# Norms, value projections and a modulation group around the layer boundary of a two-layer diffusion mixer

## The chip, the cores and the metric

The kernel runs on one core of a Trainium2 chip. The metric is the device time of one execution in microseconds (us), taken as the median over runs. Engines by their short names: PE is TensorE's matmul, PEld its weight load, DVE is VectorE, ACT is ScalarE, POOL is GpSimd, SP is SyncE, which here only issues transfers (DMAs).

## The reference, cut to what matters

Two layers, 512 tokens of 1024 channels (four tiles of 128 tokens; tiles 0 and 1 are context, 2 and 3 latent). Each layer is a token mixer (latent attention beside a chunkwise mLSTM, then an output projection) and a mixture of experts (MoE), each with a residual and a norm behind it:

```python
for l in range(DEPTH):
    sh1, sc1, g1, sh2, sc2, g2 = split(silu(c) @ w_ada[l] + b_ada[l], 6)
    y = token_mixer(layer_norm(x) * (1 + sc1) + sh1, ...)
    x = layer_norm(ALPHA * x + g1 * y, ln1_g, ln1_b)
    y = hier_moe(layer_norm(x) * (1 + sc2) + sh2, ...)
    x = layer_norm(ALPHA * x + g2 * y, ln2_g, ln2_b)
```

So between layer 0's MoE and layer 1's mixer every tile is normalised twice: by the post-norm ln2, and by the norm without gains that opens the next mixer. In the mixer the normalised input h is multiplied by columns of w_in; among them are 256 columns called kr here (keys' rest, rotary part and gates), 512 of the mLSTM's values (mv), its keys and queries (mk, mq), and others (kd, qd, po, gates of the branches). The gates of the mLSTM need the kr columns of all tiles.

## The kernel before

All is f32; products with w_in are made of three matmuls on high and low parts (`mm3`), for which weights and activations are split: the high part by a Copy on ACT, the low part by a subtraction (`sub`, L157) that goes to POOL each third time and to DVE otherwise (`split_sb`, L162; `wsplit`, L452, for weights). One tile of tokens by 256 columns takes 24 matmuls (`tm`, L537); `cm` (L547) gives 128 columns by all tokens.

The program's planner orders the instructions of each engine at build time, by their place in the text and by when a simulated operand and buffer are there; only PE's order in the MoE loop is as written. Each engine and each DMA queue then works in order. Weights pass through the W slots: four of 1 MB in the pool `wp`, taken whole by `wm` (L207) or as two halves by `w` (L198); in the MoE `wm` goes round these four and seven more (W2, layer 0) of the MoE's own pool. Tiles with tag `u` (34 in layer 1) and `hT` belong to the mixer's pool, whose memory the MoE's pool used before; `st` (12) and `pm` (4) are there for the whole program.

The end of the MoE (`moe`, L1548 to L1575): ln2's gains are loaded into a `wm` slot; for each tile in turn the combine adds the last experts (L1466, L1469, with sums), the mean is formed (L1560), `stats` (L1475) squares on ACT (L1480, result into the MoE's tile xr) and makes the inverse root on DVE: `newton` (L143) guesses through integer bits and improves three times, seven operations behind one for the argument (L1481). Two passes over the tile apply it (L1562, L1569). For layer 0 the second norm's mean and `stats` follow, and L1574 leaves r and nb. Then ada(1,1) is run (L1577), a third of layer 1's modulation: `ada(l, g)` (L355) loads 16 pieces of w_ada (L377), makes 32 products on PE (L381; 64 rows of the trace), adds a bias (L387) and stores the rows (L392). `late` means whole W slots and an order of loads as written.

The start of layer 1's mixer (L484 to L514): the kr columns are loaded and split, ada(1,2) is begun, and for each tile ACT makes xn (L492), PE turns it (L495), scale and shift are put on (L508, L510), h is split (L511, L512), and one eighth of ada(1,2) is done. After this come kr's products for all tiles (L559), the gates' first part, mk and mq (L567), the values (`mv_cols`, L582) while the gates' second part runs, and then the mLSTM (`mlstm`, L848) in ten steps, into which `weave` puts the other columns (`fill`) and, in layer 0 only, ada(0,1) and ada(0,2) (`fill2`, L670).

Of the kernel before, what the change touches and what calls it, by code (L numbers as in the profile page):

```python
# [16 lines left out]
D = 1024  # L17
NCTX = 256
T = 512
NT = 4  # L20
# [63 lines left out]
class Kern:  # L84
# [77 lines left out]
    def split_sb(self, src, name="s", weights=False):  # L162

        n = 1
        for s in src.shape[1:]:
            n *= s
        pn = src.shape[0]
        hi, lo = self.pair(n, name, weights)

        def view(t):  # L170
            v = t[0:pn]
            if len(src.shape) == 3:
                v = v.rearrange("p (a b) -> p a b", a=src.shape[1])
            return v

        self.nc.scalar.activation(view(hi), src, AF.Copy)  # L176
        self.sub(view(lo), src, view(hi).bitcast(F32))
        return view(hi), view(lo)
# [134 lines left out]
    def setup(self):  # L313
# [25 lines left out]
        self.ada_d = [self.dp.tile([2, 6 * D], F32, name=f"ada{l}") for l in range(L)]  # L339
        self.zeros = self.cp.tile([128, 1], F32, name="zeros")  # L340
# [14 lines left out]
    def ada(self, l, g, late=False):  # L355

        nc, I = self.nc, self.I
        wv = I["w_ada"][l].rearrange("(p k) n -> k p n", k=8)
        ps = self.ps("d")

        def bias():
            bt = self.pm(name="bada") if late else (self.u(name="bada") if first else self.w("bada")[:, 0:512])
            for c in range(4):
                a = g * 2048 + c * 512
                nc.sync.dma_start(out=bt[32 * c:32 * c + 32], in_=I["b_ada"][l, a:a + 512].partition_broadcast(32))
            return bt

        first = l == 0 and g == 0
        bt = bias() if first else None
        for kb in range(8):  # L370
            if late:
                t = self.wm("wada")
                wt = self.halves2(t)
            else:
                wt = [self.w("wada") for c in range(2)]
            for c in range(2):
                d = nc.sync.dma_start(out=wt[c], in_=wv[kb][:, g * 2048 + c * 1024:g * 2048 + c * 1024 + 1024])  # L377
                if late:
                    self.tc.keep_in_program_order(d)
            for c in range(4):  # L380
                nc.tensor.matmul(ps[32 * c:32 * c + 32], lhsT=self.sT[:, kb],  # L381
                                 rhs=wt[c // 2][:, (c % 2) * 512:(c % 2) * 512 + 512],
                                 start=(kb == 0), stop=(kb == 7))
            if kb < 7:
                yield
        bt = bias() if bt is None else bt
        nc.vector.tensor_tensor(out=bt, in0=ps, in1=bt, op=OP.add)  # L387
        if g == 0:
            self.ada_cols(l, bt)
        for r in range(2):  # L390
            dst = self.ada_d[l][r:r + 1, g * 2048:g * 2048 + 2048].rearrange("o (c n) -> (o c) n", c=4)
            (nc.gpsimd if l else nc.sync).dma_start(out=dst, in_=bt[r:128:32])  # L392
        yield
# [58 lines left out]
    def wsplit(self, vs, cols=None):  # L452

        res = []
        for v in vs:
            if cols is not None:
                v = v[:, :, cols]
            nk, n = v.shape[1:]
            step = 512 // n
            for k in range(0, nk, step):  # L460
                m = min(step, nk - k)
                h, lo = self.split_sb(v[:, k:k + m], "ws", True)
                res += [(h[:, i], lo[:, i]) for i in range(m)]
        return res

    def mixer(self, l):
# [10 lines left out]
        hl = mp.tile([128, 8, 512], F32R, tag="hT", name="hTl", bufs=2)  # L477
        xT = {}
        if l == 0:
            ada0 = self.ada(0, 0)  # L480
            next(ada0)
        else:

            vkr = self.load_cols(win, 512, 160, (2208, 96))  # L484
            wkr = self.wsplit(vkr)
            ada0 = self.ada(1, 2)
        for t in range(NT):
            r, nb = self.nlx[t] if l else self.ln_scale(self.X[t])
            ts = slice(t * 128, t * 128 + 128)
            for g in range(2):  # L490
                xn = (self.u if l else self.st)(name="xn")
# [21 lines left out]
                next(ada0)  # L513
        run(ada0)  # L514
        if l == 0:
            tc.keep_in_program_order(nc.sync.dma_start(out=self.cst, in_=I["cst"][:, C_CAPF:]))
# [20 lines left out]
        def tm(v, toks, ws=None):  # L537

            ws = ws or self.wsplit(v)
            n = v[0].shape[2]  # L540
            for t in toks:
                p = self.ps("g")
                s = slice(t * 128, t * 128 + 128)
                self.mm3(p[:, 0:n], [(hh[:, k, s], hl[:, k, s], ws[k][0], ws[k][1]) for k in range(8)])
                yield t, p

# [9 lines left out]
        krg = self.sm([128, NT, 48], "krg", bufs=1)  # L556
        kd2 = [self.u(name="kd") for i in range(2)]
        kd = {t: kd2[t // 2][:, (t % 2) * 256:(t % 2) * 256 + 256] for t in range(NT)}
        for t, p in tm(vkr, range(NT), wkr):  # L559
            nc.scalar.activation(kd[t][:, 128:256], p[:, 0:128], AF.Copy)  # L560
            nc.vector.tensor_copy(krg[:, t], p[:, 128:176])
# [5 lines left out]
        for dst, c0, t0, n, sc in ((mk, 928, 0, T, 1.0), (mq, 672, q0, nq, 0.125)):  # L567
            v = self.load_cols(win, c0, 256)
            for b in range(2):
# [6 lines left out]
        V1 = [mp.tile([128, self.UW], F32, tag="u", name="v1", bufs=self.NU).rearrange("p (a b) -> p a b", a=NT)  # L576
              for h in range(4)]
        tpo = [self.u(name="tpo").rearrange("p (a b) -> p a b", a=4) for h in range(4)]
        for h in range(4):
            nc.gpsimd.memset(V1[h][:, :, 128:129], 1.0)  # L580

        def mv_cols():  # L582
            for c in range(2):
                v = self.load_cols(win, 1184 + c * 256, 256)
                for t, p in tm(v, range(NT)):
                    for i in range(2):
                        nc.scalar.activation(V1[2 * c + i][:, t, 0:128], p[:, i * 128:i * 128 + 128], AF.Copy)
                    yield
# [70 lines left out]
        for _ in range(4):  # L659
            next(fill)  # L660
# [9 lines left out]
        fill2 = self.chain(*[self.ada(0, g) for g in (1, 2)]) if l == 0 else iter(())  # L670
        mlstm = self.mlstm(l, QT, gates, mq, mk, V1, tpo, hmT)
        self.weave(mlstm, 10, [(fill, 32 if last else 34), (fill2, 16)])
# [611 lines left out]
    def moe(self, l):  # L1284
# [190 lines left out]
        def stats(X, nm, eps):  # L1475

            v, a, r = (self.ss_tile([128, 2], x) for x in "var")
            q, v, a, r = v[:, 1:2], v[:, 0:1], a[:, 0:1], r[:, 0:1]
            xi[0] += 1
            nc.scalar.activation(xrs[xi[0] % 3], X, AF.Square, bias=nm, accum_out=q)  # L1480
            nc.vector.tensor_scalar(v, q, 0.5 / D, 0.5 * eps, op0=OP.mult, op1=OP.add)  # L1481
            self.newton(r, v, a)
# [65 lines left out]
        ln2 = self.wm("ln2")  # L1548
# [4 lines left out]
        sums = {t: sm([128, 3], "sum", bufs=n) for t in QT}  # L1553
        comb = combine(done, sums)
        for t in QT:
# [4 lines left out]
            nc.vector.tensor_scalar(nm, sums[t][:, 0:1], sums[t][:, 1:2], -1.0 / D, op0=OP.add, op1=OP.mult)  # L1560
            r = stats(X, nm, EPS / ALPHA ** 2)
            nc.vector.scalar_tensor_tensor(X, X, nm, lg, op0=OP.add, op1=OP.mult)  # L1562
            if last:
# [4 lines left out]
                continue  # L1568
# [3 lines left out]
            nc.vector.tensor_scalar(nm, s2, -1.0 / D, None, op0=OP.mult)  # L1572
            r = stats(X, nm, EPS)
            nc.vector.tensor_tensor(out=nb, in0=nm, in1=r, op=OP.mult)  # L1574
            self.nlx[t] = (r, nb)  # L1575
        if not last:
# [19 lines left out]
```

## Time and profile before

| | |
|---|---|
| median of 3 runs | 1433.42 us (1429.83 to 1434.53) |
| the profiled execution | 1433.49 us, its span 1431.7 us |
| mean granted clock of TensorE | 0.947 |
| busy: PE, DVE, ACT, POOL | 1290.5, 798.3, 450.0, 379.9 us |
| moved by DMA | 339.66 MB, mean 237 GB/s |
| one w_ada piece, one wide w_in piece | 512 KB each |

The span is from the first to the last instruction; times in rows count from its start. Layer 0's mixer runs to some 530, its MoE to 826, layer 1's mixer to some 1150, its MoE to the end. In rows of windows the busy times come in the order PE, PEld, DVE, ACT, POOL; a clock of 1.00 is 2.4 GHz, 0.50 is 1.2 GHz. In timelines a row can stand for several equal instructions (x count), and brackets hold the idle time before it and what ended it. A matmul's length in the rows is modelled and overlaps the next one; distances between starts say more.

### The profile page before, as it was taken

The numbers are of one execution on the slowest core, as the hardware profiler recorded it, in microseconds if no ns is written. First come the engines' busy times: TensorE is split into PE (matmuls) and PEld (weight loads), VectorE is DVE, ScalarE is ACT, GpSimd is POOL, SyncE is SP. The second block draws the span as 40 slices with busy tenths as digits, with TensorE's granted clock in tenths as the row PEclk, the third lists the DMA queues.
The fourth block names the chain that finished last, engine by engine and source line by source line (L and its number), as shares of the span: only waits on it lengthen the run. The fifth ranks groups of instructions, "written<-read, shape, count | busy, mean of one in ns | idle before, by whom it ended". The sixth has DMA issues, their size and how long they took to land. (4 is left out here: it accounts for less than half of the span.)

```text
span 1431.7 us, 19677 instructions
## 1 busy us (share of the span) xinstructions
PE 1290.5 (90%) x6839; PEld 832.9 (58%) x6839; DVE 798.3 (56%) x2197; ACT 450.0 (31%) x998; POOL 379.9 (27%) x389
## 2 busy tenths in 40 slices
PE   5799999999999837899999969999999749999995
PEld 1688866776776633434454516998878634444442
DVE  2645777553236955555554486478775863343325
ACT  3434344343340102111121127356545212121121
POOL 1410114100342402444343312112524401232222
PEclk9999999999999958999999979999999959999998
DMA  9634454311257376979999968321444768999994
GB/s 327 205 96 148 140 200 126 99 44 60 89 176 269 131 289 228 404 278 409 408 407 409 404 211 281 96 79 40 152 143 133 232 252 329 408 408 407 407 408 156
DMA packets 146036, 339.66 MB, mean 237 GB/s; under 512 B 21552, under 2 KB 67792, under 8 KB 145920
## 3 DMA queue, kind: packets, MB, share of 16 engines
q1 hardware_dynamic: 137376, 322.87, 61.8%
q0 software_dynamic: 6096, 10.05, 2.0%
q10 hardware_dynamic: 2448, 5.31, 1.1%
q8 instruction: 59, 0.97, 0.3%
q14 instruction: 57, 0.47, 0.1%
HBM read 344.62 MB, written 4.29 MB: 244 GB/s over the span
## 5 line engine op out<-in xcount | busy, mean ns | idle before, releaser
L1426 PE MATMUL ps_g<-we,xs 128*64 128x512 f32 x992 | 240.1, 609 | 6.5 <-DMA we<-in_w_e_up 4.2
L160 POOL TENSOR_TENSOR wsl<-wc,wsh 128x512 fp32r<-128x512 f32 x55 | 73.9, 1346 | 326.9 <-ACT wsh L176 287.1
L1426 PEld LDWEIGHTS ps_g<-we,xs 128*64 128x64 f32 x992 | 75.3, 140 | 145.7 <-issue 139.0
L1472 POOL TENSOR_TENSOR X<-X,acc 128x512 f32<-128x512 f32 x96 | 125.1, 1326 | 110.2 <-DVE acc L1466 110.2
L160 DVE TENSOR_TENSOR wsl<-wc,wsh 128x512 fp32r<-128x512 f32 x107 | 86.8, 815 | 98.2 <-ACT wsh L176 78.2
L176 ACT ACTIVATE wsh<-wc 128x512 fp32r<-128x512 f32 x162 | 99.0, 628 | 120.3 <-PE ps_g L197 81.3
L1430 DVE SCALAR_TENSOR_TENSOR si<-si,ws,ps_g 128x256 f32<-128x256 f32 (+1 forms) x33 | 15.8, 480 | 205.6 <-ACT si L1429 205.6
L1449 PE MATMUL ps_a<-we,hidT 128*64 128x512 f32 x496 | 125.6, 595 | 3.2 <-DMA we<-in_w_e_down 3.1
L196 PE MATMUL ps_g<-wsh,hTh 128*128 128x256 f32 x400 | 115.2, 290 | 6.1 <-ACT hTh L533 3.1
L1382 POOL DMA_INDIRECT xr<-h2d,ti x33 | 34.8, 1055 | 312.2 <-PE ps_t L1394 203.6
L198 PE MATMUL ps_g<-wsh,hTl 128*128 128x256 f32 x400 | 113.3, 286 | 4.2 <-DVE hTl L160 4.1
L196 PE MATMUL ps_g<-hTh,wsh 128*128 128x512 f32 (+1 forms) x320 | 112.8, 352 | 1.9 <-ACT tg L627 1.9
L197 PE MATMUL ps_g<-wsl,hTh 128*128 128x256 f32 x400 | 113.7, 286 | 0.0
L197 PE MATMUL ps_g<-hTl,wsh 128*128 128x512 f32 (+1 forms) x320 | 111.1, 347 | 0.0
L198 PE MATMUL ps_g<-hTh,wsl 128*128 128x512 f32 (+1 forms) x320 | 110.4, 345 | 0.0
L381 PE MATMUL ps_d<-wada,sT 128*32 128x512 f32 x380 | 69.1, 641 | 30.4 <-DMA wada<-in_w_ada 15.4
L1466 DVE TENSOR_TENSOR acc<-ps_d,g 128x512 f32<-128x512 f32 x108 | 74.0, 689 | 38.1 <-PE ps_d L1464 24.3
L1429 ACT ACTIVATE si<-ps_g 128x256 f32<-128x256 f32 (+1 forms) x33 | 12.7, 384 | 241.5 <-PE ps_g L1426 186.4
L1463 PE MATMUL ps_d<-yh,pmr 128*128 128x512 f32 (+1 forms) x200 | 83.2, 417 | 1.2 <-DVE acc L1466 0.9
L196 PEld LDWEIGHTS ps_g<-wsh,hTh 128*128 128x128 f32 x400 | 76.6, 192 | 13.3 <-ACT hTh L533 3.4
L1449 PEld LDWEIGHTS ps_a<-we,hidT 128*64 128x64 f32 x496 | 38.4, 137 | 77.7 <-issue 61.0
L1464 PE MATMUL ps_d<-yl,pmr 128*128 128x512 f32 (+1 forms) x200 | 79.4, 398 | 0.9 <-DVE yl L190 0.9
(404 smaller groups left out, 2677.3 us busy)
## 6 DMA issues: line engine op xcount, KB each, us to landing
we<-in_w_e_gate SPq DMA_DIRECT2D x124, 512.0 KB, 10.2
we<-in_w_e_up SPq DMA_DIRECT2D x124, 512.0 KB, 10.5
we<-in_w_e_down SPq DMA_DIRECT2D x124, 512.0 KB, 10.2
wada<-in_w_ada SPq DMA_DIRECT2D x95, 512.0 KB, 6.5
wc<-in_w_in SPq DMA_DIRECT2D x63, 512.0 KB, 4.7
wc<-in_w_out SPq DMA_DIRECT2D x16, 512.0 KB, 5.7
wc<-in_w_bo_mla SPq DMA_DIRECT2D x8, 512.0 KB, 4.7
wc<-in_w_bo_mlstm SPq DMA_DIRECT2D x6, 512.0 KB, 3.5
```

The lines of the kernel that those rows point to most:

```text
L160: eng.tensor_tensor(out=out, in0=a, in1=b, op=OP.subtract)
L176: self.nc.scalar.activation(view(hi), src, AF.Copy)
L196: self.nc.tensor.matmul(out, lhsT=ah, rhs=bh, start=(i == 0), stop=False)
L197: self.nc.tensor.matmul(out, lhsT=ah, rhs=bl, start=False, stop=False)
L198: self.nc.tensor.matmul(out, lhsT=al, rhs=bh, start=False, stop=(i == n - 1))
L381: nc.tensor.matmul(ps[32 * c:32 * c + 32], lhsT=self.sT[:, kb], rhs=wt[c // 2][:, (c % 2) * 512:(c % 2) * 512 + 512], start=(kb == 0), sto ...
L1426: nc.tensor.matmul(p[64 * e:64 * e + 64], lhsT=xs[:, k, 64 * e:64 * e + 64], rhs=W[e, k], start=(k == 0), stop=(k == 7))
L1449: nc.tensor.matmul(p[64 * e:64 * e + 64], lhsT=hT_[:, c, 64 * e:64 * e + 64], rhs=W[e, c, h], start=(c == 0), stop=(c == 1))
L1463: nc.tensor.matmul(p, lhsT=lt, rhs=yh[h][0:m], start=(j == 0), stop=False)
L1464: nc.tensor.matmul(p, lhsT=lt, rhs=yl[h][0:m], start=False, stop=(j == len(parts) - 1))
L1466: nc.vector.tensor_tensor(out=a, in0=p, in1=g2[t // 2][h], op=OP.mult)
L1472: nc.gpsimd.tensor_tensor(out=X, in0=X, in1=a, op=OP.add)
```

## The change

- Roots: `stats` takes Sqrt on ACT, then a reciprocal and two DVE operations (one Newton step) in place of the guess and three steps. Its squares go to a bf16 tile of tag `st`.
- The norms become a generator for each tile (`norm`), in steps. In layer 0's MoE only the first steps are called; the others are called in the next mixer, between the starts of the tiles. For this ln2 lies in a W slot of `wp` and the sums in a lasting pool, and xn takes `st` tiles.
- In layer 1, kr's and the values' columns are loaded at the start, the values' sixteen split tiles lie in `u` with all low parts on POOL, and each tile's kr and value products follow its own start (`from_start`). `mv_cols` then does nothing in layer 1.
- ada(1,2) is taken from the start of the mixer and woven into the mLSTM as `fill2`, eight steps over ten. The bias loads of the late ada(1,1) are issued by POOL.

```diff
-    def split_sb(self, src, name="s", weights=False):
+    def split_sb(self, src, name="s", weights=False, pool=False):
...
-        self.sub(view(lo), src, view(hi).bitcast(F32))
+        if pool:
+            self.nc.gpsimd.tensor_tensor(out=view(lo), in0=src, in1=view(hi).bitcast(F32), op=OP.subtract)
+        else:
+            self.sub(view(lo), src, view(hi).bitcast(F32))
...
+        self.eps = {}
+        for e in (EPS, EPS / ALPHA ** 2):
+            self.eps[e] = self.cp.tile([128, 1], F32, name=f"eps{len(self.eps)}")
+            nc.gpsimd.memset(self.eps[e], e)
...
-                nc.sync.dma_start(out=bt[32 * c:32 * c + 32], in_=I["b_ada"][l, a:a + 512].partition_broadcast(32))
+                (nc.gpsimd if late else nc.sync).dma_start(out=bt[32 * c:32 * c + 32],
+                                                           in_=I["b_ada"][l, a:a + 512].partition_broadcast(32))
...
-                h, lo = self.split_sb(v[:, k:k + m], "ws", True)
+                h, lo = self.split_sb(v[:, k:k + m], "ws", not far, far)
...
+        def start_tiles():
+
+            k2 = [self.u(name="kd") for i in range(2)]
+            V1.extend(mp.tile([128, self.UW], F32, tag="u", name="v1", bufs=self.NU).rearrange("p (a b) -> p a b", a=NT)
+                      for h in range(4))
+            for h in range(4):
+                nc.gpsimd.memset(V1[h][:, :, 128:129], 1.0)
+            return (self.sm([128, NT, 48], "krg", bufs=1),
+                    {t: k2[t // 2][:, (t % 2) * 256:(t % 2) * 256 + 256] for t in range(NT)}, k2)
+
+        def kr_out(t, p):
+            nc.scalar.activation(kd[t][:, 128:256], p[:, 0:128], AF.Copy)
+            nc.vector.tensor_copy(krg[:, t], p[:, 128:176])
+
+        def mv_out(c, t, p):
+            for i in range(2):
+                nc.scalar.activation(V1[2 * c + i][:, t, 0:128], p[:, i * 128:i * 128 + 128], AF.Copy)
...
-            wkr = self.wsplit(vkr)
-            ada0 = self.ada(1, 2)
+            krg, kd, kd2 = start_tiles()
+            vv = [self.load_cols(win, 1184 + c * 256, 256) for c in range(2)]
-        for t in range(NT):
+        def start(t):
...
-                xn = (self.u if l else self.st)(name="xn")
+                xn = self.st(name="xn")
...
-                next(ada0)
-        run(ada0)
+        def from_start(t):
+            kr_out(t, next(tm(vkr, [t], wkr))[1])
+            for c in range(2):
+                mv_out(c, t, next(tm(vv[c], [t], wmv[c]))[1])
         if l == 0:
+            for t in range(NT):
+                start(t)
+        else:
+            def norm(*ts):
+                for t in ts:
+                    next(self.norms[t])
+            norm(0)
+            wkr = self.wsplit(vkr)
+            start(0)
+            norm(2, 1)
+            wmv = [self.wsplit(v, None, True) for v in vv]
+            start(1)
+            from_start(0)
+            norm(3, 2)
+            start(2)
+            from_start(1)
+            norm(3)
+            start(3)
+            from_start(2)
+            from_start(3)
+        if l == 0:
+            run(ada0)
...
-            for c in range(2):
+            for c in range(0 if l else 2):
...
-        fill2 = self.chain(*[self.ada(0, g) for g in (1, 2)]) if l == 0 else iter(())
+        fill2 = self.chain(*[self.ada(0, g) for g in (1, 2)]) if l == 0 else self.ada(1, 2)
         mlstm = self.mlstm(l, QT, gates, mq, mk, V1, tpo, hmT)
-        self.weave(mlstm, 10, [(fill, 32 if last else 34), (fill2, 16)])
+        self.weave(mlstm, 10, [(fill, 32 if last else 34), (fill2, 8 if last else 16)])
...
-            q, v, a, r = v[:, 1:2], v[:, 0:1], a[:, 0:1], r[:, 0:1]
-            xi[0] += 1
-            nc.scalar.activation(xrs[xi[0] % 3], X, AF.Square, bias=nm, accum_out=q)
-            nc.vector.tensor_scalar(v, q, 0.5 / D, 0.5 * eps, op0=OP.mult, op1=OP.add)
-            self.newton(r, v, a)
+            q, v, a, r0, r = v[:, 1:2], v[:, 0:1], a[:, 0:1], r[:, 0:1], r[:, 1:2]
+            junk = self.cp.tile([128, 1024], BF16, tag="st", name="junk", bufs=self.NST)
+            nc.scalar.activation(junk, X, AF.Square, bias=nm, accum_out=q)
+            nc.scalar.activation(r0, q, AF.Sqrt, scale=1.0 / D, bias=self.eps[eps])
+            nc.vector.tensor_scalar(v, q, -0.5 / D, -0.5 * eps, op0=OP.mult, op1=OP.add)
+            nc.vector.reciprocal(r0, r0)
+            nc.vector.tensor_scalar(a, r0, v, r0, op0=OP.mult, op1=OP.mult)
+            nc.vector.scalar_tensor_tensor(r, a, 1.5, r0, op0=OP.add, op1=OP.mult)
...
-        ln2 = self.wm("ln2")
+        ln2 = self.wp.tile([128, 2048], F32, tag="W", name="ln2", bufs=self.NW)
...
-        sums = {t: sm([128, 3], "sum", bufs=n) for t in QT}
+        sums = {t: self.ss_tile([128, 2, 6], "st")[:, 0] for t in QT}
...
-        for t in QT:
+        def norm(t):
             for h in range(2):
                 next(comb)
             X = self.X[t]
             nm, s2 = self.ss_tile([128, 4], "mv")[:, 0:1], sums[t][:, 2:3]
             nc.vector.tensor_scalar(nm, sums[t][:, 0:1], sums[t][:, 1:2], -1.0 / D, op0=OP.add, op1=OP.mult)
+            yield
             r = stats(X, nm, EPS / ALPHA ** 2)
             nc.vector.scalar_tensor_tensor(X, X, nm, lg, op0=OP.add, op1=OP.mult)
             if last:
...
                     hs = slice(h * 512, h * 512 + 512)
                     nc.vector.scalar_tensor_tensor(X[:, hs], X[:, hs], r, lb[:, hs], op0=OP.mult, op1=OP.add)
                     nc.sync.dma_start(out=self.out[0, (t - 2) * 128:(t - 1) * 128, hs], in_=X[:, hs])
-                continue
+                yield
+                return
             nc.vector.scalar_tensor_tensor(X, X, r, lb, op0=OP.mult, op1=OP.add, accum_out=s2)
             nm, nb = self.ss_tile([128, 4], "mv")[:, 0:1], self.ss_tile([128, 1], "nb")
             nc.vector.tensor_scalar(nm, s2, -1.0 / D, None, op0=OP.mult)
+            yield
             r = stats(X, nm, EPS)
             nc.vector.tensor_tensor(out=nb, in0=nm, in1=r, op=OP.mult)
             self.nlx[t] = (r, nb)
+            yield
+        self.norms = {t: norm(t) for t in QT}
+        for t in (2, 2, 3, 3) if last else (0, 1, 0, 2, 1, 3):
+            next(self.norms[t])
         if not last:
             self.drain(self.ada(1, 1, True))
             self.half = None
```

## Rows read from the trace of the kernel before

**Rows 1.** windows, four stretches: range, length, busy by engine (instructions), clock, DMA share, GB/s

```profile
107.00:143.00 36.00, 36.00 (x258) 29.35 (x256) 20.77 (x81) 17.64 (x60) 2.55 (x2) 1.00 0.43 147
823.00:859.00 36.00, 21.81 (x112) 5.18 (x110) 31.24 (x101) 10.51 (x19) 4.36 (x4) 0.76 0.60 211
931.00:967.00 36.00, 36.00 (x280) 32.99 (x280) 25.88 (x96) 18.27 (x53) 5.69 (x4) 1.00 0.27 85
1217.00:1253.00 36.00, 36.00 (x174) 15.00 (x172) 13.05 (x43) 6.89 (x15) 9.36 (x8) 1.00 1.03 408
```

**Rows 2.** the chain of waits, in order of time: start, length, what

```profile
1179.71 9.27 PE ps_g L1426 x32
...
1190.34 9.71 DMA we<-in_w_e_up
```

**Rows 3.** timeline of PE at the boundary: start, length, line, operation

```profile
826.15 7.07 PE L381 MATMUL ps_d<-wada,sT 128*32 128x512 f32 x64
...
860.93 1.36 PE L495 MATMUL ps_t<-ident,xn 128*128 128x128 f32 x8 [0.61 <-ACT xn L492]
...
867.76 0.40 PE L196 MATMUL ps_g<-wsh,hTh 128*128 128x256 f32 x1 [0.16 <-ACT hTh L511]
...
886.72 0.28 PE L198 MATMUL ps_g<-wsh,hTl 128*128 128x256 f32 x1
```

**Rows 4.** timeline of ACT, boundary to the first mLSTM weights

```profile
825.12 1.15 ACT L1480 ACTIVATE xr<-X,ln_mv 128x1024 f32<-128x1024 f32 x1 [6.39 <-DVE ln_mv L1560]
...
860.08 4.32 ACT L492 ACTIVATE xn<-X,ln_nb,ln_r 128x512 f32<-128x512 f32 x6
...
887.73 1.28 ACT L788 ACT_TABLE_LOAD   x1
...
919.34 0.20 ACT L845 ACTIVATE em<-ps_t 128x32 f32<-128x32 f32 x1 [0.31 <-DVE uT L844]
...
927.67 0.45 ACT L587 ACTIVATE v<-ps_g 128x128 f32<-128x128 f32 x2 [2.37 <-PE ps_g L198]
...
930.48 0.45 ACT L587 ACTIVATE v<-ps_g 128x128 f32<-128x128 f32 x2 [0.89 <-PE ps_g L198]
```

**Rows 5.** windows at the boundary and under the gates (columns as rows 1)

```profile
834.00:842.00 8.00, 5.29 (x16) 0.75 (x16) 6.46 (x25) 3.06 (x5) 0.00 (x0) 0.62 0.63 239
...
900.00:910.00 10.00, 8.24 (x64) 7.52 (x62) 8.80 (x15) 1.82 (x4) 0.68 (x6) 1.00 0.54 168
910.00:920.00 10.00, 9.39 (x65) 9.27 (x65) 4.43 (x10) 4.39 (x14) 2.50 (x2) 0.83 0.00 0
```

**Rows 6.** timeline of DVE at the boundary

```profile
824.88 0.21 DVE L1560 TENSOR_SCALAR ln_mv<-sum 128x1 f32<-128x1 f32 x1
...
838.61 0.15 DVE L1574 TENSOR_TENSOR ln_nb<-ln_mv,ln_r 128x1 f32<-128x1 f32 x1
...
846.19 1.77 DVE L160 TENSOR_TENSOR wsl<-wc,wsh 128x512 fp32r<-128x512 f32 x1
...
848.25 0.67 DVE L160 TENSOR_TENSOR wsl<-wc,wsh 128x512 fp32r<-128x512 f32 x1
...
860.20 0.15 DVE L1481 TENSOR_SCALAR ln_v<-ln_v 128x1 f32<-128x1 f32 x1 [1.37 <-ACT xr L1480]
...
862.09 0.16 DVE L1574 TENSOR_TENSOR ln_nb<-ln_mv,ln_r 128x1 f32<-128x1 f32 x1
```

**Rows 7.** timeline of DVE, end of the program

```profile
1426.67 1.42 DVE L1566 SCALAR_TENSOR_TENSOR X<-X,ln_r,ln 128x512 f32<-128x512 f32 x2
```

**Rows 8.** timeline of POOL at the boundary

```profile
844.29 3.12 POOL L160 TENSOR_TENSOR wsl<-wc,wsh 128x512 fp32r<-128x512 f32 x2 [0.78 <-ACT wsh L176]
```

**Rows 9.** timeline of SP's DMA issues

```profile
797.72 19.78 SPq L377 DMA_DIRECT2D wada<-in_w_ada  x16
...
831.27 29.00 SPq L377 DMA_DIRECT2D wada<-in_w_ada  x16
```

**Rows 10.** who waited for whom, 820 to 885: total us, times, longest

```profile
PEld ps_d L381 <- DMA wada<-in_w_ada: 27.0, 12, 12.1
```

More of the change, by code (lines that the diff above doesn't have):

```diff
@@ L450, in load_cols, with wsplit @@
         return res
-    def wsplit(self, vs, cols=None):
+    def wsplit(self, vs, cols=None, far=False):
         res = []
@@ L477, in mixer, with tm @@
         hl = mp.tile([128, 8, 512], F32R, tag="hT", name="hTl", bufs=2)
+        def tm(v, toks, ws=None):
+            ws = ws or self.wsplit(v)
+            n = v[0].shape[2]
+            for t in toks:
+                p = self.ps("g")
+                s = slice(t * 128, t * 128 + 128)
+                self.mm3(p[:, 0:n], [(hh[:, k, s], hl[:, k, s], ws[k][0], ws[k][1]) for k in range(8)])
+                yield t, p
+        def start_tiles():
[12 more added lines that the diff above has]
+                nc.scalar.activation(V1[2 * c + i][:, t, 0:128], p[:, i * 128:i * 128 + 128], AF.Copy)
+        V1 = []
         xT = {}
@@ L535, in mixer @@
                 self.dump(f"h{k}", h)
[L537 to L545, printed above, removed]
         def cm(v, b, toks0, n):
@@ L553, in cm @@
             return p
[L556 to L561, printed above, removed]
+        if l == 0:
+            krg, kd, kd2 = start_tiles()
+            for t, p in tm(vkr, range(NT), wkr):
+                kr_out(t, p)
         gen = self.gates(l, krg[:, :, 32:48])
@@ L575, in mixer @@
                     next(gen)
-        V1 = [mp.tile([128, self.UW], F32, tag="u", name="v1", bufs=self.NU).rearrange("p (a b) -> p a b", a=NT)
-              for h in range(4)]
         tpo = [self.u(name="tpo").rearrange("p (a b) -> p a b", a=4) for h in range(4)]
-        for h in range(4):
-            nc.gpsimd.memset(V1[h][:, :, 128:129], 1.0)
         def mv_cols():
-            for c in range(2):
+            for c in range(0 if l else 2):
                 v = self.load_cols(win, 1184 + c * 256, 256)
                 for t, p in tm(v, range(NT)):
-                    for i in range(2):
-                        nc.scalar.activation(V1[2 * c + i][:, t, 0:128], p[:, i * 128:i * 128 + 128], AF.Copy)
+                    mv_out(c, t, p)
                     yield
@@ L659, in mixer @@
         for _ in range(4):
-            next(fill)
+            next(fill, None)
         gates = next(gen)
```

## The prediction

> **What bounds the kernel now.** I read the windows of all engines first. In most of the mixers TensorE is the bound: 36.00 of 36 us busy at clock 1.00, both in layer 0 and in layer 1 [rows 1]. In layer 1's expert loop it is the DMA engines, at 408 GB/s and a share of 1.03 [rows 1]. Between the layers, from 823 to 859, nothing is saturated: PE 21.81 of 36 us, clock 0.76, DMA 0.60, while DVE is busy for 31.24 us [rows 1]. The chain that ended last reaches back only to the start of layer 1's expert loop (32 first-tile matmuls at 1179.71, then one weight load after another from 1190.34) [rows 2]. The load stream starts when the mixer and the routing let it, and then runs at its rate; so a mixer that ends earlier by x moves the end by x.
>
> So the stretch to read is the boundary. PE leaves the last combine at 826.2, runs ada(1,1) in 7.07 us, and then is fed by loads and waits; the first projection (L196) starts at 867.76, the last of the 96 of vkr at 886.72 [rows 3]. From 826.2 to 886.8 lie 60.6 us. The work in them at full clock is 2 x 7.07 for ada(1,1) and ada(1,2), 32 transposes at 1.36 per 8 = 5.4, four vkr tiles and 13 matmuls of mk. A tile of 24 matmuls takes 2.81, the distance between the value copies at 927.67 and 930.48 [rows 3, 4], so vkr is 11.2 us; the 13 have twice the columns, some 3.0. Sum 33.7; **27 us are waste**: waits and half clock (0.62 of full from 834 to 842, which is mostly the 1.2 GHz level) [rows 5].
>
> Why PE waits is seen on DVE and ACT. Tile 0's second norm is finished at 838.61, but ACT starts its xn only at 860.08, six in a row, behind the Square of the last tile; tile 3's norm ends at 862.09 [rows 4, 6]. ACT had room: three tiles were ready and not begun. In after the norm's buffers (junk, ln2, sums, xn) lie outside the pool that has to close for the mixer, and the norm of tile t+2 stands behind the start of tile t in the text.
>
> **The parts.**
>
> *Roots.* Eight of these norms lie at the boundary, two in the tail. Today each takes eight small dependent DVE operations; the last, undisturbed, needs 862.09 - 860.20 = 1.9 us [rows 6]. After it is a Sqrt on ACT, and behind it reciprocal and two operations. No row shows Sqrt; the nearest is the Exp of 128x32 at 0.20 us [rows 4]. With two hand-overs and three DVE operations of 0.15 to 0.27 I take 1.2 us (bounds 0.8 and 1.9): 0.7 less in each chain. Against that stand table loads. Square, Copy and Identity run here after Silu's or Exp's table without a load, so I count one more at the boundary (Silu to Sqrt, then Exp as now) and one in the tail. A load takes 1.28 us [rows 4], mostly in ACT's idle time. The Trainium skill (ScalarE: Activation LUTs, What ACT_TABLE_LOAD costs) speaks against this part: it gives 2.66 us a switch, as a drain comes on top. In this trace the operation behind the load at 887.73 waits for DVE, so that row can't settle the drain. By the page, two loads on the path would cost 2.8 us more and the sum would be 1424.3. In the tail, DVE's last normalising pair starts at 1426.67 behind two interleaved Newton chains [rows 7]; 2 x 0.7 less and partly the load more: 0.7 us gained (bounds -1 and 1.5).
>
> *Staggering.* Tile 0's mean is there at 824.88, its first Square starts at 825.12 [rows 4, 6]. The bare chain is two Squares with their sums (1.3 each), two roots (1.2), a table load, one normalising pass and small ones: nb at some 832.5. Before, DVE crowded with combines, it took until 838.61 [rows 6]. I take 835. From xn to the first projection it was 7.7 us (860.08 to 867.76) with six xn in a row [rows 3, 4]; bare it is some 5. I take 6: **first projection at 841**, bounds 837.5 and 846.3.
>
> *Values per tile.* Eight tiles of 24 matmuls, 8 x 2.81 = 22.5 us, move from under the gates to the boundary. Their 16 splits were there before; now all eight lows go to POOL. POOL runs such a pair in 3.12 us [rows 8], so eight take some 12 us from when the columns have landed; they must be done before the first values tile is. These subtractions also slow DVE: a DVE subtraction took 1.77 us beside POOL's and 0.67 alone [rows 6, 8]. Eight such meetings cost DVE up to 8 x 1.1 = 9 us (below: 0, when it is then idle). DVE's own work from 824 to the last tile's low part I count at some 38 us by its kinds; with the contention 38 to 47, so the last tile comes at 862 to 871 and has 8.4 us of projections to go. PE, from 841, has 5.4 + 12 x 2.81 = 39.1 us and ends at 880 if it never waits. The two are level, so I add 3 us of mutual waits (0 to 6) and 2.5 for half clock after the stop (0 to 4).
>
> Sum for the boundary: work 7.1 + 39.1 = 46.2, waste 841 - 833.2 = 8, plus 3 and 2.5: 13.5 us, end at 886. **Waste goes from 27 to 13.5: 13.5 gained**, as PE's work is otherwise the same.
>
> *Last modulation woven later.* ada(1,2) has 16 loads, which occupied SP from 831.27 for 29.00 us [rows 9]; mk's columns queue no longer behind them. Its 7.07 us of PE and one 0.69 us addition are in the sum already, as they are only moved; its four bias loads and two stores go along. What covers it: layer 0 weaves two such groups into the same generator, and its windows show PE at 36.00 of 36 [rows 1]. So zero for stalls; without that cover see the rivals.
>
> *Gates.* Their chain ran from some 887.7 to 919.5 (em) under mk, mq and four or five values tiles [rows 4]; even so PE was short of work, 8.24 of 10 us and 9.39 at clock 0.83 [rows 5]. The tiles that stood there are gone; kd's, qd's and po's columns can be drawn ahead, as they need no gate. I take 3 us lost (bounds -2, when the old gap goes, and 14).
>
> *Small.* Four bias loads of ada(1,1) leave SP for POOL: some 0.6 us each on POOL, before the value lows; vkr's columns pass on SP. V1's memsets only move, two memsets for eps lie under the first loads. Free, unless POOL then waits with the lows behind a late ada(1,1): up to 7 us, in the first rival.
>
> **Sum.** 13.5 - 3 + 0.7 = 11.2, say 12 with SP's freed queue (mk's columns land before they are wanted). The profiled execution took 1433.49 for a span of 1431.7, 0.07 above the median. Forecast 1421.5.
>
> **Rivals.**
>
> 1. *The slots.* ln2 now holds one of the four W slots through the last tile, and ada(1,1)'s eight blocks want four W in turn. Its 16 loads today go out from 797.72 within 19.78 us without a stop [rows 9]. After, the fourth block may wait until PE frees the first at 827, and vkr and values are behind it on SP: ten loads of ada, vkr and two value groups are 8.4 MB, 20.6 us at 408 GB/s [rows 1], so vkr lands at 843, the values at 848, their lows end at 857. PE would start at 845.5 and end near 890; waste 17 to 18, time 1426. For it: the count of slots. Against: a PE gap could take the first block early.
>
> 2. *Gates uncovered.* If no other columns are drawn ahead, some 12 us of values are missing there, and the clock falls as at 910 to 920 [rows 5]: 16 instead of 3, time 1435. It decides from a gap of 10 us on.
>
> 3. *Not staggered.* If xn of tile 0 is still put behind the last norm, now near 855, the first projection is at 862 and 39 us follow, without ada(1,2) to fill the wait: done at 904. Today's order, with 22.5 for values added and ada's 7.1 and mk's 3.0 taken off, stands there at 886.8 + 12.4 = 899. Some 5 us slower: 1439. It decides when xn comes later than 850. For it: that is what the trace shows now. Against: the buffers that could cause it have been moved out.
>
> 4. *ada(1,2) starves the mixer*, on the slower side. Its loads and the columns share four W slots. At the boundary PE's weight side waited for wada 12 times, 27.0 us [rows 10], 2.25 each. Eight blocks that each stop PE so cost 18 us: 1439.5. It decides above 16 us, 2 per block. Against: layer 0's full windows.
>
> **Numbers.** Forecast 0.48 (its own range 1412 to 1429, from the bounds of first projection, waits and gates, not all at one end), slots 0.20, gates 0.12, not staggered 0.10, starved 0.10. A measurement of this kernel can tell about 0.3%, 4.3 us: below 1429.1 is faster, above 1437.7 slower. Faster: 0.48 + 0.17 + 0.02 = 0.67. Same: 0.03 + 0.07 + 0.02 + 0.02 = 0.14. Slower: 0.03 + 0.08 + 0.08 = 0.19. The range goes from 1412 to 1437 and leaves out most of the last two rivals and some 3 in 100 below.
>
> **What would show it.** Right: tile 0's xn before 838 and its projection near 841, value copies (L587's) between the tiles' kd copies, no stretch of PE idle over 8 us after 833, ada's matmuls inside the mLSTM at 0.11 us each without DMA waits, Sqrt with one table load ahead of it. Wrong: late wada loads on SP after 826 (rival 1), a PE gap between mq and the first mLSTM weights (2), six or more xn in a row behind a Square (3), waits for wada after 930 (4). If TensorE's windows from 930 on are no longer full, the mixer is bound by DVE and the moved matmuls buy nothing.

## The result, and the profile after

The changed kernel takes 1453.32 us (1447.31 to 1454.44, 4 runs) against 1433.97 (1429.83 to 1436.49, 4 runs) of the kernel before on the same chip: ratio 1.0126, 95% interval 1.0101 to 1.0152. It is slower, by some 19 us, where 12 less were forecast, and lies outside the range. The profiled execution has a span of 1452.3 us.

Layer 0 is the same up to 800. Four places differ after it.

SP's issues after, and who SP waited for (795 to 850; total us, times, longest):

```profile
797.92 35.73 SPq L385 DMA_DIRECT2D wada<-in_w_ada  x16
835.22 12.75 SPq L456 DMA_DIRECT2D wc<-in_w_in  x8
...
SPq L385 <- PE ps_d L389: 18.4, 1, 18.4
```

In [rows 9] the 16 issues of ada(1,1) took 19.78 us; now 35.73, with one wait of 18.4 for products that free a slot. vkr's columns stand behind them and are issued from 835.22.

ACT's timeline after:

```profile
827.01 0.18 ACT L1528 ACTIVATION_READ_ACCUMULATOR junk<-X,ln_mv 128x1 f32 x1
827.22 1.28 ACT L1529 ACT_TABLE_LOAD   x1
828.51 0.29 ACT L1529 ACTIVATE ln_r<-ln_v,eps 128x1 f32<-128x1 f32 x1
...
847.18 1.15 ACT L176 ACTIVATE wsh<-wc 128x512 fp32r<-128x512 f32 x2 [8.98 <-DMA wc<-in_w_in]
...
850.00 1.50 ACT L530 ACTIVATE xn<-X,ln_nb,ln_r 128x512 f32<-128x512 f32 x2
...
864.85 1.52 ACT L530 ACTIVATE xn<-X,ln_nb,ln_r 128x512 f32<-128x512 f32 x2 [5.17 <-DVE ln_nb L1630]
```

Tile 0's norm was ready at 839.1, but in ACT's order its xn stands behind the split of vkr, which waits 8.98 us for its load: 850.00, where 835 was forecast. Tile 1's xn then waits 5.17 us for DVE. The norms are staggered, then, but late.

PE after:

```profile
826.99 2.78 PE L389 MATMUL ps_d<-wada,sT 128*32 128x512 f32 x24
...
845.26 1.05 PE L389 MATMUL ps_d<-wada,sT 128*32 128x512 f32 x4 [0.35 <-DMA wada<-in_w_ada]
...
857.13 0.58 PE L199 MATMUL ps_g<-wsh,hTh 128*128 128x256 f32 x1 [4.32 <-ACT hTh L549]
...
861.96 0.58 PE L201 MATMUL ps_g<-wsh,hTl 128*128 128x256 f32 x1 [3.60 <-DVE hTl L160]
```

The first projection is at 857.13 (forecast 841; 867.76 in [rows 3]), the last of the boundary near 905 (forecast 886). The windows, columns as rows 1:

```profile
850.00:860.00 10.00, 3.19 (x12) 2.50 (x12) 8.37 (x15) 9.68 (x21) 5.92 (x5) 0.50 0.89 290
860.00:870.00 10.00, 8.04 (x49) 8.05 (x50) 6.87 (x13) 5.15 (x10) 6.70 (x5) 0.65 0.51 159
...
940.00:950.00 10.00, 9.02 (x34) 7.07 (x34) 8.70 (x30) 5.01 (x18) 1.27 (x1) 0.60 0.49 156
```

PE is short of work twice: where the tiles start, and again at 940 to 950, behind the gates (em at 937.61, 919.34 in [rows 4]), at a granted clock of 0.60, close to the 1.2 GHz level.

Last, in front of the router, ACT's queue, first of the kernel before, then after:

```profile
1152.58 2.33 ACTq L749 DMA_DIRECT2D h2d<-h  x2
1155.02 1.09 ACT L263 ACTIVATE h2T<-ps_a 128x512 f32<-128x512 f32 x2 [8.04 <-PE ps_a L261]
```

```profile
1169.37 7.52 ACTq L797 DMA_DIRECT2D h2d<-h  x2
1176.99 1.08 ACT L266 ACTIVATE h2T<-ps_a 128x512 f32<-128x512 f32 x2 [13.35 <-DMA we<-in_w_e_up]
```

The issue of two stores, not touched by the change, takes 7.52 us, and the router's copies stand behind it.

### The profile page after: what moved, and what is told of

It is laid out like the page before. It is cut to its first block, busy times and chain, and to the rows that moved or that the text cites. A ratio compares the mean times of both kernels' runs of the same rounds, so it can differ in the third digit from the quotient of the medians.

```text
span 1452.3 us, 19631 instructions
## 1 busy us (share of the span) xinstructions
PE 1304.7 (90%) x6839; PEld 841.6 (58%) x6839; DVE 790.8 (54%) x2152; ACT 454.2 (31%) x1010; POOL 391.5 (27%) x400
## 5 line engine op out<-in xcount | busy, mean ns | idle before, releaser
L389 PE MATMUL ps_d<-wada,sT 128*32 128x512 f32 x380 | 72.2, 618 | 22.2 <-DMA wada<-in_w_ada 22.2
L1477 ACT ACTIVATE si<-ps_g 128x256 f32<-128x256 f32 (+1 forms) x33 | 12.7, 384 | 239.3 <-PE ps_g L1474 183.7
L201 PEld LDWEIGHTS ps_g<-wsh,hTl 128*128 128x128 f32 x400 | 78.0, 197 | 7.7 <-DVE hTl L160 7.4
```

The lines of the kernel that those rows point to most:

```text
L201: self.nc.tensor.matmul(out, lhsT=al, rhs=bh, start=False, stop=(i == n - 1))
```

## The experiments

Times are medians; the kernel before had 1433.8 to 1434.9 beside them. Times of two traces can't be compared to the microsecond: y1 and z2 below differ only in an edit behind the boundary, and yet their first Square of tile 0 starts at 827.94 and 823.76 (825.12 before, 825.96 in the changed kernel). Where it matters, times are counted from this Square.

**Four parts, one by one.** The turn of the slots moved on, so that the late ada does not want ln2's (x1); ada(1,2) woven and nothing else (x2); the roots alone (x3); x1 with the values under the gates, as before (x4).

```diff
+        self.wi += 1
```

> The changed kernel, with one step more in the turn of wm behind ln2, so that ada(1,1) asks for three W slots as before and not for four. Theory S (the 18.4 us for which SP stands at the fourth block is the main loss, as vkr's columns and with them ACT's whole order wait for it): ada(1,1)'s sixteen loads go out without a stop by 818, vkr lands by 836, the first xn comes before 842 instead of 850.0, and the time is 1441 to 1445 (9 to 12 us under the changed kernel's 1453). Theory G (the loss arises under the gates and in the mLSTM, which lost their cover): the boundary gets better, but what is gained there is lost behind it, and the time stays within 3 us of 1453.

Measured 1447.22 (ratio 1.0088, 1.0063 to 1.0112): 6.1 less than the change, between the two theories. The slot is a part, and not the whole. Tile 0's xn comes at 838.67 now, but the first projection no sooner than in the changed kernel (857.13), with DVE stopped for 3.83 us between them; v1 below comes back to this stop.

```profile
838.67 1.51 ACT L530 ACTIVATE xn<-X,ln_nb,ln_r 128x512 f32<-128x512 f32 x2
...
847.78 3.83 DVE L1631 TENSOR_TENSOR ln_nb<-ln_mv,ln_r 128x1 f32<-128x1 f32 x1
...
857.22 0.58 PE L199 MATMUL ps_g<-wsh,hTh 128*128 128x256 f32 x1
```

```diff
-            ada0 = self.ada(1, 2)
...
-        fill2 = self.chain(*[self.ada(0, g) for g in (1, 2)]) if l == 0 else iter(())
+        fill2 = self.chain(*[self.ada(0, g) for g in (1, 2)]) if l == 0 else self.ada(1, 2)
...
```

> The kernel before with only ada(1,2) moved into the mLSTM's weave. If its matmuls lay in PE's idle time at the boundary and now lie where PE is full, the time rises by their length, 7 to 9 us, to 1441 to 1443 (theory M: moved from free to bound). If PE's work only changes places and the boundary ends earlier by as much, as the prediction's sum had it, it stays within 2 us of 1433.5. If its loads starve the mixer it goes to 1448 or more.

Measured 1450.74 (1.0108, 1.0085 to 1.0131), 15.9 slower: this step alone loses most of what the change loses. By its size it lies where the loads were expected to starve the mixer; w2 and w3 below test that. The first product of mk comes at 883.6 (882.4 before), so taking ada(1,2) from the boundary gained nothing there. In the mLSTM PE stays full, in contrast to a starved mixer:

```profile
920.00:940.00 20.00, 20.00 (x156) 18.54 (x156) 5.87 (x17) 7.42 (x25) 0.99 (x1) 1.00 0.34 106
940.00:960.00 20.00, 20.00 (x143) 15.47 (x143) 10.43 (x49) 9.50 (x30) 2.63 (x2) 1.00 0.45 156
```

PE's timeline in x2 shows why it still loses:

```profile
899.57 1.04 PE L381 MATMUL ps_d<-wada,sT 128*32 128x512 f32 x2
900.55 0.39 PE L196 MATMUL ps_g<-hTh,wsh 128*128 128x256 f32 x1
...
941.80 1.04 PE L381 MATMUL ps_d<-wada,sT 128*32 128x512 f32 x2
942.78 0.39 PE L196 MATMUL ps_g<-wsh,hTh 128*128 128x256 f32 x1
```

One product (two rows) between other work takes 0.98 us from its start to the next one's. Back to back, [rows 3] have 64 rows in 7.07: 0.88 for four products, which fill the four 32-row quarters of the output side by side. The planner has put the 32 products in 14 pieces, each a run of products without other work between; from each start to the next operation they add up to 16.1 us, a wait of 1.38 among it. The loss is 15.9.

```diff
-            self.newton(r, v, a)
+            nc.scalar.activation(r0, q, AF.Sqrt, scale=1.0 / D, bias=self.eps[eps])
...
```

> The kernel before with only the roots changed to Sqrt on ACT. If xn waits for the last norm, as in the trace of before, eight chains shortened by 0.7 us each bring it forward by 4 to 6 us, and the tail gives 1: 1427 to 1429. If table loads and hand-overs cost what the shorter chains give, it stays within 1.5 us of 1433.5; by the table load's price on the path alone (1.28 twice) it is at most 2.6 us slower.

Measured 1435.74 (1.0006, 0.9991 to 1.0022): no difference. In its trace the first projection comes 2.7 us sooner behind the first Square than before (39.98 against 42.64), but em only 0.4 (93.86 against 94.22): what the shorter roots gain at the boundary is gone by the end of the gates.

```diff
-            vv = [self.load_cols(win, 1184 + c * 256, 256) for c in range(2)]
...
-            for c in range(0 if l else 2):
+            for c in range(2):
```

> As x1_slots, but the values are projected where they were, under the gates; staggered norms, roots and the woven ada(1,2) stay. Theory G: the gates get their cover back, the half clock and the sparse stretch behind the first mLSTM weights go, and it is 5 to 10 us faster than x1_slots. Theory S alone: the values' 22.5 us of PE are then missing in the boundary's gaps, and it is 3 to 10 us slower than x1_slots.

Measured 1438.47 (1.0028, 1.0011 to 1.0045), 8.8 less than x1: the values cost time where the change puts them.

**ada(1,2) back at the boundary**, among the starts of the tiles, in x4 (y1) and in x1 (y2):

```diff
+            ada0 = self.ada(1, 2)
             norm(0)
...
                 self.sub(ol, h, oh.bitcast(F32))
+                next(ada0)
...
```

> x4_values_late with ada(1,2) taken out of the mLSTM and put back among the starts of the tiles; staggered norms and ScalarE's roots stay. Theory P (the woven ada costs the TensorE time of its pieces on a stretch that is full, and was free where TensorE waited): the 14 pieces of about 1 us leave the mLSTM and lie in the waits of the boundary (7.2 and 6.8 us in x4): 12 to 16 less than x4's 1438.5, so 1423 to 1427, faster than before. Rival B (with the norms staggered the boundary has no room left, every piece delays the projections, and its loads stand in front of the columns): 1434 or more. If the staggering is worth nothing by itself, it gives the time of before, 1434.

> x1_slots (the whole change, with the slot that ln2 holds no longer in the turn) with ada(1,2) put back among the starts of the tiles; the values stay projected per tile there. Theory P: 12 to 16 less than x1's 1447.2, so 1431 to 1436. Rival B: the boundary is now filled by the values, ada's eight loads stand among theirs and delay them: 1443 or more. By the theory on the values (they cost some 9 us as they are missing under the gates) it is 7 to 10 slower than y1.

y1 takes 1426.45 (0.9945, 0.9925 to 0.9965), 12.0 less than x4 and faster than before. y2 takes 1441.51 (1.0050, 1.0033 to 1.0068): only 5.7 less than x1, between the two theories, probably as the values leave less room there. y2 less y1 is 15.1, the values' price in this setting, where 7 to 10 were expected.

**Fewer pieces.** In y3 and y4 the four products of a block are kept together (in x2 and in x4); in z1 x2's ada(1,2) is drawn ahead of the mLSTM's steps, so that its products stand in 7 pieces.

```diff
+            with self.tc.tile_critical() if (l, g) == (1, 2) else ExitStack():
...
+        if last:
+            run(fill2)
```

> x2_ada_only (before with ada(1,2) woven into the mLSTM and nothing else) with the four products of a block of w_ada kept together, so 8 pieces where x2 has 14; loads, slots and places of the blocks as in x2. Theory P: a piece of one to four products takes the same 0.98 us, so 8 pieces take some 8 us where 14 took 14.6: 1442 to 1445 against x2's 1450.7. Theory Q (not TensorE's time but the loads, that take W slots and SP's queue from the mixer's columns): no change, 1449 to 1452.

> x4_values_late with the four products of a block kept together, as y3. Theory P: 6 to 8 less than x4's 1438.5: 1430.5 to 1433. Theory Q: as x4, 1437 to 1440.

> x2_ada_only with ada(1,2) drawn in one go ahead of the mLSTM's ten steps, so that its 32 products stand in 7 pieces (2, 1, 3, 6, 4, 1 and 15 products) where x2 has 14, without any wait added; otherwise before. Theory P (a piece of one to four products takes 0.98 us of TensorE on a full stretch): five pieces at 0.98, one of two rows of four at 1.85 and one of four rows at some 3.7, together 10.5 where x2 has 14.6, and they can fill part of the 2.5 us stop under the gates: 1443 to 1447 against x2's 1450.7. Theory Q (loads, slots and SP's queue): the loads now stand in front of the gates' columns, 1451 or more.

Measured 1457.58, 1444.10 and 1453.22: all slower than what they start from, so all three missed. Keeping products together made PE wait for other engines first, once for 4.14 us:

```profile
996.93 1.94 PE L382 MATMUL ps_d<-wada,sT 128*32 128x512 f32 x8 [4.14 <-DVE hmT L190]
```

In z1 the seven pieces add up to 10.3 us (10.5 expected), but PE was short of work elsewhere, at a granted clock of 0.83 and 0.91 where x2 had 1.00:

```profile
940.00:960.00 20.00, 17.96 (x110) 13.94 (x103) 7.41 (x21) 6.09 (x18) 2.43 (x3) 0.83 0.78 251
960.00:980.00 20.00, 18.72 (x126) 16.56 (x126) 12.31 (x54) 7.96 (x26) 3.17 (x2) 0.91 0.16 54
```

None of them decides between PE's time and the loads. The next two do: on the kernel before, ada(1,2)'s loads once more in the mLSTM without products (w2), and as many products from a tile in memory without loads (w3). The planner put w3's products sooner than x2's, from 876.93 to 923.32, ahead of the mLSTM.

```diff
+                nc.sync.dma_start(out=wt[c], in_=wv[kb][:, 4096 + c * 1024:4096 + c * 1024 + 1024])
+                nc.gpsimd.tensor_copy(self.ss_tile([128, 1], "nb"), wt[c][:, 0:1])
```

> Before, with eight steps woven into layer 1's mLSTM that load the sixteen pieces of w_ada once more, at the place where the change puts ada(1,2), and let GpSimd copy one column of each, so that the slots come free; no products with them (ada(1,2) itself stays at the start; the loaded copies are not used). Theory P (the products' time on a full TensorE is the price): within 4 of 1434. Theory Q (slots and SP's queue): 1444 to 1451.

```diff
+                nc.tensor.matmul(ps[32 * c:32 * c + 32], lhsT=self.sT[:, kb],
+                                 rhs=self.X[c // 2][:, (c % 2) * 512:(c % 2) * 512 + 512],
+                                 start=(kb == 0), stop=(kb == 7))
```

> Before, with 32 further products of the shape of ada(1,2)'s woven into layer 1's mLSTM, from a tile that is in memory, so without a load; their result is copied once and not used. They stand in 10 pieces, early. Theory P: nine pieces at 0.98 and one of fourteen products at some 3.6, 12.4 us, less what falls into the stop under the gates (2.5): 1444 to 1447. Theory Q: within 4 of 1434.

Loads alone: 1435.47 (1.0005, 0.9992 to 1.0018), nothing. Products alone: 1445.57 (1.0082, 1.0061 to 1.0102), 11.5 slower in 10 pieces, which take 12.4. The price is PE's time; four pieces more at 0.98 would bring w3's 11.5 to some 15.4 (an estimate), close to x2's 15.9. In w2 GpSimd lets a slot go once its load has landed, so a slot that is held until PE comes isn't tested by it. w3's PE rows, a piece of one product and one of two:

```profile
879.92 1.04 PE L401 MATMUL ps_d<-X,sT 128*32 128x512 f32 x2
880.90 0.39 PE L198 MATMUL ps_g<-wsh,hTl 128*128 128x256 f32 x1
...
886.74 1.05 PE L401 MATMUL ps_d<-X,sT 128*32 128x512 f32 x4
887.72 0.39 PE L196 MATMUL ps_g<-wsh,hTh 128*128 128x256 f32 x1
```

**The stores of h2** issued by GpSimd in layer 1: in y1 (z2), in the whole change (z3), in before (z5) and in y2 (w1).

```diff
-                    nc.scalar.dma_start(out=self.h2_d[l]
+                    (nc.gpsimd if l else nc.scalar).dma_start(out=self.h2_d[l]
```

> y1_values_late_ada_start with the two stores of h2 in layer 1 issued by GpSimd's queue instead of ScalarE's. Theory R (the store's issue is held on ScalarE's queue behind the expert loads, and the copies of h2T and the router stand behind it): y1's pair of issues took 2.89 us, before's 2.33; without it ScalarE copies at once: 1.5 to 3 less than y1, 1423.5 to 1425. If the transposes or the loads set the router's start, as y1, 1426.5.

> The whole change with the two stores of h2 in layer 1 issued by GpSimd's queue. Theory R: the pair of issues took 7.52 us in the changed kernel against 2.33 in before, and the router's last product came 5.4 later than the out-projection's delay explains: 5 to 7 less than 1453, so 1446 to 1448. If the expert loads set it: within 2 of 1453.

> Before with the two stores of h2 in layer 1 issued by GpSimd's queue, the control to y1 with z2 and the changed kernel with z3. If the store's hold is the change's own doing (before's pair of issues took 2.33 us against 7.52): at most 1 to 2.5 less than 1434, within what can be told. If the same move gains 3 or more here, the store is a cost of both kernels and explains less of the difference.

> y2_slots_ada_start (all of the change but the woven ada and the slot) with the two stores of h2 in layer 1 issued by GpSimd's queue. y2's pair of issues took 7.81 us. If the values' cost (y2 less y1: 15.1) is partly that hold: 6 to 8 less than y2's 1441.5, 1433.5 to 1435.5, and the values by themselves cost 10 to 12 (against z2's 1423.25). If the hold is only a shift: 1439 or more.

z2 takes 1423.25 (0.9916, 0.9898 to 0.9934), z3 1444.86 (1.0066, 1.0050 to 1.0082), w1 1435.91 (1.0011, 0.9999 to 1.0023): 3.2, 8.5 and 5.6 less than the same kernel with ACT's issue (expected: 1.5 to 3, 5 to 7, 6 to 8). On before it is 1432.16 (0.9990, 0.9977 to 1.0003): not to be told from nothing. The pair of issues takes 7.52, 7.60 and 7.81 us in the changed kernel, x1 and y2, 2.33 in before and 1.81 to 3.11 in the ten other kernels that leave it to ACT. So the long hold belongs to the variants with the values at the boundary. Why an issue is held so long is not shown; in the slow cases SP issues four expert loads within the same two microseconds (from 1169.50 in the changed kernel).

**The roots again**, now in y1, which has the norms staggered: z4 is y1 with Newton's steps on DVE.

> y1_values_late_ada_start with the inverse roots by DVE's Newton steps as in before (x3 had the roots alone and showed no difference); the norms stay staggered. If the staggering alone gives y1's gain and ScalarE's roots give nothing: within 2 of y1's 1426.5. If the roots shorten the chain now that it lies ahead of the first projection, 0.7 for each of two roots and the crowding of DVE with it: 1429 to 1433.

1432.36 (0.9984, 0.9968 to 0.9999), 5.9 more than y1: ACT's roots are worth nothing in the old order and some 6 us in the staggered one. Only 1.2 of this is there at the first projection (25.54 us behind the first Square, against 24.34 in y1), and all of it at the second tile's router (330.74 against 324.81): most of the gain arises behind the boundary, and by what isn't shown.

**The values' low parts** on DVE instead of GpSimd, in w1:

```diff
-            self.nc.gpsimd.tensor_tensor(out=view(lo), in0=src, in1=view(hi).bitcast(F32), op=OP.subtract)
+            self.nc.vector.tensor_tensor(out=view(lo), in0=src, in1=view(hi).bitcast(F32), op=OP.subtract)
```

> w1_values_start_h2_by_pool with the sixteen low parts of the values' columns subtracted by DVE instead of GpSimd; nothing else moved. In w1 tile 1's nb, an operation of 0.15 us, took 3.83 beside GpSimd's three subtractions, and ScalarE's xn of tile 1 waited 5.03 for it. Theory D (that blocking of DVE by GpSimd's subtractions is most of the values' 12.7 us against z2): the sixteen cost DVE some 0.67 each, 10.7 in all, partly idle time; 1426 to 1431 against w1's 1435.9. Rival U (what costs is that 22.5 us of products stand ahead of the gates and are missing under them): within 3 of 1435.9, or slower, as DVE's own queue grows.

1429.48 (0.9970, 0.9956 to 0.9984), 6.4 less than w1. There are eight such low parts of 128x512 and not sixteen: GpSimd subtracts three, three, one and one in w1's trace, and DVE eight times in v1's, some 5.4 us in all. w1's DVE, POOL, ACT and PE, a timeline each:

```profile
849.16 3.83 DVE L1634 TENSOR_TENSOR ln_nb<-ln_mv,ln_r 128x1 f32<-128x1 f32 x1
...
849.26 3.70 POOL L178 TENSOR_TENSOR wsl<-wc,wsh 128x512 fp32r<-128x512 f32 x3
...
853.03 1.52 ACT L530 ACTIVATE xn<-X,ln_nb,ln_r 128x512 f32<-128x512 f32 x2 [5.03 <-DVE ln_nb L1634]
...
857.92 0.62 ACT L549 ACTIVATE hTh<-h 128x512 fp32r<-128x512 f32 x1
...
860.72 0.58 PE L199 MATMUL ps_g<-wsh,hTh 128*128 128x256 f32 x1
```

and the same operations in v1:

```profile
849.30 0.15 DVE L1634 TENSOR_TENSOR ln_nb<-ln_mv,ln_r 128x1 f32<-128x1 f32 x1
...
849.55 0.63 ACT L549 ACTIVATE hTh<-h 128x512 fp32r<-128x512 f32 x1 [0.97 <-ACT wsh L176]
850.08 1.50 ACT L530 ACTIVATE xn<-X,ln_nb,ln_r 128x512 f32<-128x512 f32 x2
...
851.65 0.58 PE L199 MATMUL ps_g<-wsh,hTh 128*128 128x256 f32 x1
```

A product of one column by one column takes 3.83 us while GpSimd subtracts three times, and ACT waits for it with all that stands behind. PE's first projection is at 860.72 in w1 and at 851.65 in v1; 1.2 us of this lie ahead of the first Square (825.83 and 824.67), and 7.9 are left. The planner also ordered ACT anew: tile 0's hTh, which the projection needs, stands behind tile 1's xn in w1 and ahead of it in v1. So the 6.4 us go with the engine of the subtractions, by the stop and by the order around it together; how they divide isn't shown. The Trainium skill (SBUF — State Buffer, Who interferes with whom) says that a DVE instruction with two SBUF inputs contends with a GpSimd instruction that reads SBUF, over shared ports that one of them holds exclusively. The rows agree: the DVE operation ends at 852.99, as the third subtraction does (852.96).

## Why the prediction was wrong

**The account.** From the change to the best version the runs go 1453.32, less 6.1 for the slot (x1), less 5.7 for ada(1,2) back at the boundary (y2), less 5.6 for the store (w1), less 12.7 for the values back under the gates (z2): 1423.25. What then is left of the change, staggered norms with ACT's roots, and the store moved, is 11.3 faster than the 1434.53 of before beside it. In this order the values are the largest part, and three terms of the forecast failed: the modulation, the slots and the values; the store was in none. The price of a part hangs on what stands beside it: ada(1,2) is worth 15.9 on before, 12.0 in x4 and 5.7 in x1.

**"So zero for stalls", "as they are only moved".** This is the first step of the prediction that failed. The 7.07 us were taken from a row in which the products run back to back and counted on both sides of the sum. At the boundary they had cost nothing, since PE waited there anyway (x2), and in the mLSTM they cost 16, as split pieces on a full engine. The windows named as cover, 36.00 of 36 [rows 1], were the argument against: where PE is full, a moved product is paid in full. That a product costs nearly 1 us there could be read from the kernel before, in layer 0:

```profile
146.23 1.04 PE L381 MATMUL ps_d<-wada,sT 128*32 128x512 f32 x2
147.21 0.70 PE L881 MATMUL ps_a<-mqk 64*128 64x256 f32 x2
```

The fourth rival had the right part and nearly the right price (18 us), but by waits for loads, for which w2 shows nothing.

**The slots.** The first rival was right in its mechanism: the wait for a slot is there, 18.4 us on SP. It priced it at 4.5 us over the forecast; x1 shows 6.1. ACT's order is what it missed: tile 0's xn, long ready, stands behind the split of the late columns. Nor is the gain where it had it: x1's first projection is as late as the changed kernel's.

**Staggering: first projection at 841.** Without the values and the slot, this is z2:

```profile
823.76 1.15 ACT L1527 ACTIVATE junk<-X,ln_mv 128x1024 bf16<-128x1024 f32 x1 [6.40 <-DVE ln_mv L1613]
...
834.43 1.15 ACT L1527 ACTIVATE junk<-X,ln_mv 128x1024 bf16<-128x1024 f32 x1 [5.88 <-DVE ln_mv L1627]
...
837.98 1.51 ACT L529 ACTIVATE xn<-X,ln_nb,ln_r 128x512 f32<-128x512 f32 x2
...
848.10 0.38 PE L199 MATMUL ps_g<-wsh,hTh 128*128 128x256 f32 x1 [0.17 <-ACT hTh L548]
```

That xn is "before 838" is luck of this trace, whose first Square is 1.4 us sooner than before's. From the first Square xn comes after 14.2 us (also in y1, x1 and x4), where the forecast had 835 - 825.12 = 9.9: the Square of the second norm waits 5.88 us for DVE. From xn to the projection it is 10.1 where 6 were taken; between the two, ACT's order has Squares, roots and tile 1's xn. So the projection comes 24.3 us behind the Square, before 42.6, forecast 15.9: the idea holds, and some 8 us of its gain were an error of size. Rival 3's reason, xn behind the last norm, is in no trace with the staggered norms, though the changed kernel's xn at 850.00 lies at its bound.

**Values per tile.** The waits were taken as 3 us at the boundary and 3 under the gates; together the values cost 12.7 (w1 to z2). Half, 6.4, goes with the subtractions' engine (v1). The prediction had seen the slowing, but priced it at 1.1 us a meeting, from a subtraction that took 1.77 instead of 0.67 [rows 6, 8], and as load on DVE, not as a stop in the chain of norms. The other 6.2 are not settled: v1's first projection still comes 2.6 us later behind the first Square than z2's, and v1 has PE at a granted clock of 0.85 and 0.81 from 930 to 950, about the end of its gates (em at 932.35), where z2 has 1.00. The latter speaks for the second rival, but no run separates that.

**Roots and tail.** 0.7 us for each chain gave nothing alone (x3) and, with the staggering, 5.9 (y1 against z4): the forecast took a fixed size for a term that depends on the order around it. The table load began at 827.22, right behind the end of the read before it (827.19), took 1.28 us, and the Sqrt began at 828.51, so a switch costs 1.3 us here. This settles the question left in the forecast: the 2.66 us that the Trainium skill (ScalarE: Activation LUTs, What ACT_TABLE_LOAD costs) gives for it do not show. The tail's 0.7 is not shown: from the second tile's router to the end it is 276.0 us before and 274.7 after, but 275.7 in x3, which has the roots alone, and 276.1 and 277.9 in y1 and z2, which have them too; z4, with Newton's steps, has 276.0.

**The store** was in no step. It was on ACT's queue in the trace of before, at 2.33 us for two. What makes its issue long isn't shown.

## What to carry to other kernels

A piece of work that is "only moved" has two prices, one at each place. Here it was free where its engine waited, and where its engine was full it cost all its time, at the price that it had when it was split among other work. So read the row of such a piece in the stretch it goes to. And a subtraction that is given to an idle GpSimd can stop a chain of one-column operations on DVE that is worth more than the subtraction.

## What the runs showed of the hardware

Four products on 32 rows each, side by side in one output tile, take 0.88 us when eight such groups stand back to back; one to four of them between other products take 0.97 to 1.00 each time. A DVE operation of 0.15 us took 3.83 behind three subtractions on GpSimd. The issue of two 256 KB stores on ACT's queue took 0.99 to 1.09 us for the first tile and from 1.81 to 7.81 for the second; the same on GpSimd's took 1.21 to 1.23, with ACT's work no longer behind it.
